# Output projection of a FoX / RG-LRU block: six layer norms' row operations on ScalarE and GpSimd, and the next layer's first weights split earlier

## The chip, the cores and the metric

The kernel runs on one core of a Trainium2 chip. The metric is the time of one launch in device microseconds (us), taken from several runs; the profile is one further execution in which every engine's instructions are recorded. The engines are PE (TensorE, the matrix engine; PEld is its loading of weights), DVE (VectorE), ACT (ScalarE), POOL (GpSimd) and SP (SyncE, which issues DMAs).

## The reference, cut to what matters

One encoder block on `x` of 1024 tokens by 1024 channels, in float32:

```python
x = layer_norm(ALPHA * x + 0.5 * swiglu(x, ffn1...), ln1_g, ln1_b)
z = x @ w_in
fox = forgetting_attention(q, k, v, fg)            # 8 heads, causal, 64 wide
lru = gelu(lg) * rg_lru(causal_depthwise_conv(lx))  # 512 channels
mix = concatenate([fox, lru]) @ w_out               # 1024 x 1024
x = layer_norm(ALPHA * x + mix, ln2_g, ln2_b)       # <- the norm that is changed
x = layer_norm(ALPHA * x + 0.5 * swiglu(x, ffn2...), ln3_g, ln3_b)

def layer_norm(x, g, b):
    mu, var = mean(x, -1), mean((x - mu)**2, -1)
    return (x - mu) * rsqrt(var + 1e-5) * g + b
```

`swiglu(x)` is `(silu(x @ w_gate) * (x @ w_up)) @ w_down` with 4096 hidden channels.

## The kernel before, in words

Every float32 product is made of three matmuls on numbers split into a high and a low part (`mm3`, lines 156 to 158: high by high, high by low, low by high). A split costs a copy on ACT (the high part) and a subtraction on DVE (the low part). The gate and up products of both feed-forward layers work on 2 by 2 blocks with seven products in place of eight, so sums and differences of blocks are formed on DVE and split there as well (`first_pair` for the first pair of weight blocks, where the blocks of `x` are formed too; `weights` for the later ones).

The stretch of the change is the end of the attention and the begin of the second feed-forward layer. The row tiles `acc[i]` (128 tokens by 1024 channels; in the rows below `row`, in the program `row_5303` for tile 7 down to `row_5296` for tile 0) hold the residual. The last two heads of the attention are finished from the last query tile to the first, and as soon as two query tiles are complete, their output projection is appended to `tiles`. `out_tile` takes one half (512 channels) of a row tile from there, multiplies (PE), adds the product to the row tile (line 222, DVE), and behind the second half runs `layer_norm` and the store of the row tile to DRAM (`x2_d`, line 1166, issued by POOL). So tiles 7, 6, 5, 4, 3, 2, 1, 0 are normalized in this order, between the attention's last steps: probabilities (lines 994 to 1003), their transposes (1014 to 1019), products with the values (1030 to 1038).

`layer_norm` computes mean and variance on DVE (lines 194, 197), a row operation (line 198: minus mean, times gain), the square root on ACT (199), four operations on one column (200 to 203: one Newton step for the inverse root) and a second row operation (205: times inverse root, plus bias). The gain tile `gb[0]` holds the negative gain, and `y` leaves line 203 negative too.

After the loop over the units, the normalized tiles 4 to 7 are transposed on PE and split into the blocks `A["11"]`, `A["12"]` (`block_1`, lines 242, 247, 248) with the rest of the `out_tile` calls between them. Then `gate_up` of the second layer begins: the first blocks of the gate and up weights (`raws`, loaded by SP) are split by `fill` (line 325), the first products follow (`x` in the rows), tiles 0 to 3 are transposed (into banks `b`, line 242), copied (line 382) and so on. `g.sum` and `u.sum` are copied to SBUF at lines 366 and 385.

Each engine executes its instructions in one fixed order. A scheduler sets that order when the program is built, from the order of the code and its own estimates; so an instruction's place on its engine can move although its line did not.

Of the kernel before, what the change touches and what calls it, by code (L numbers as in the profile page):

```python
# [17 lines left out]
P = 128  # L18
# [30 lines left out]
def f32(ap):  # L49
    return ap.bitcast(F32)  # L50


class Block:
# [133 lines left out]

    def layer_norm(self, i, done=None):

        nc, v, gb = self.nc, self.nc.vector, self.gb  # L190
        a = self.acc[i]
        st = self.small.tile([P, 2, 6], F32, tag="st", name=self.nm("st"))
        for j in range(2):
            v.bn_stats(st[:, j, :], a[:, j * H:(j + 1) * H])
        s = self.small.tile([P, 8], F32, tag="ln", name=self.nm("ln"))
        mv, sd, y, w = s[:, 0:2], s[:, 2:3], s[:, 3:4], s[:, 4:5]
        v.bn_aggr(mv, st)
        v.scalar_tensor_tensor(a, a, mv[:, 0:1], gb[0], op0=ALU.subtract, op1=ALU.mult)
        nc.scalar.activation(sd, mv[:, 1:2], AF.Sqrt, bias=self.eps)
        v.tensor_scalar(w, mv[:, 1:2], EPS, 0.5, op0=ALU.add, op1=ALU.mult)  # L200
        v.reciprocal(y, sd)
        v.scalar_tensor_tensor(w, y, w, y, op0=ALU.mult, op1=ALU.mult)
        v.scalar_tensor_tensor(y, w, 1.5, y, op0=ALU.subtract, op1=ALU.mult)
        for ds in (slice(0, H), slice(H, D)) if done else (slice(0, D),):
            v.scalar_tensor_tensor(a[:, ds], a[:, ds], y, gb[1][:, ds], op0=ALU.mult, op1=ALU.add)
            if done:
                done(i, ds)
# [59 lines left out]

    def gate_up(self, wg, wu, h_d, rows, bank, tp, wsp, raws, later=None, aside=None, js=(0, 1, 2, 3)):

# [40 lines left out]
        def first_pair(g, u):  # L310
# [22 lines left out]

            homes = {(n, m): two_blocks() for n in ("11", "21", "t1") for m in both}
            t21 = [block() for _ in range(4)]
# [15 lines left out]
            else:  # L351
                for m in both:
                    fill(m, "11", q[m][0])
                do(2)
            g.sum, u.sum = self.sum_bank(), self.sum_bank()
# [9 lines left out]
            do()  # L365
            nc.scalar.copy(g.s1, g.sum)
            fill(u, "t1", t1[u])
# [13 lines left out]
            for n, j in enumerate(js):  # L381
                nc.scalar.copy(t21[j], self.transposed(r2[j], 0, bank))
                a22[j] = self.transposed(r2[j], 1, bank)
                if n == 0:
                    nc.scalar.copy(u.s1, u.sum)
                else:
                    put(place("s1", js[n - 1]), s[js[n - 1]])
                v.tensor_tensor(s[j], a22[j], t21[j], ALU.add)
                if n:
                    do()  # L390
# [569 lines left out]
    def attention(self, w_out, mixp, ln, normed):  # L960
# [7 lines left out]
        with self.pool("att_p", 3) as pp, self.pool("att_t", 1) as tp, self.pool("att_pt", 6) as ptp, self.pool("att_qk", 2, side="right") as qkp:  # L968
# [85 lines left out]
            def out_tile():  # L1054
                i, d = tiles.pop(0)
                self.down_tile(i, list(zip(mix + [mixes[3]], w_fox)), 1.0, (d,))
                if d:
                    self.layer_norm(i)
                    normed(i)
# [38 lines left out]
def kernel(  # L1098
# [40 lines left out]
    with blk.psum():  # L1139
# [32 lines left out]
        for j in range(4):  # L1172
# [3 lines left out]
            if tiles:  # L1176
                out_tile()
        while tiles:
            out_tile()
        left.close()  # L1180
    with blk.pool("xl") as xl, blk.pool("gu_t", 4) as tp, blk.banks() as bank:
        blk.open_blocks(xl, REST)
        raws, load = blk.first_raws(ffn2_w_gate[0], ffn2_w_up[0])
        with tc.issue_after(blk.last_load.ins):
            load(0)
            load(1)
        finish = blk.gate_up(ffn2_w_gate[0], ffn2_w_up[0], h_d[1], rows, bank, tp, wsp, raws, js=(3, 2, 1, 0))
    right.close()
# [41 lines left out]
```

## Time and profile before

| | before |
|---|---|
| time, median of 3 runs | 2328.83 us (2328.11 to 2330.89) |
| time of the profiled execution | 2330.4 us |
| span of the profiled execution | 2328.7 us |
| granted TensorE clock, mean | 0.999 |
| PE busy | 2302.9 us (99% of the span), 10721 matmuls |
| DVE busy | 1632.5 us (70%), 2509 instructions |
| ACT busy | 1011.1 us (43%), 1587 instructions |
| POOL busy | 222.0 us (10%), 364 instructions |

The profiled execution's time is its span and 1.7 us around it. Busy times are sums over the instructions of an engine; the ends of matmuls are modelled, so that a busy PE can still lose some tenths of a microsecond around a wait. In the groups of rows below, "idle before" and the brackets `[0.94 <-ACT ws L382]` say for how long an engine was idle ahead of an instruction and which instruction released it.

### The profile page before, as it was taken

Reading aid. Unit: us, or ns where it says so; the run is one execution under the profiler, and the core shown is the slowest. Engines: PE = TensorE matmul, PEld = TensorE weight load, DVE = VectorE, ACT = ScalarE, POOL = GpSimd, SP = SyncE. Lnnn points to the kernel's source line nnn. Section 1 sums busy time; section 2 is a strip of 40 time slices with the busy share of each in tenths; the row PEclk is TensorE's granted clock in tenths of the full one; section 3 lists DMA queues with packets and bytes.
Section 4 is the critical chain, followed back from the end, with each engine's and each line's share of the span. In section 5 each row is a group of like instructions: output and inputs, shape, how many; then the busy total and the mean of one; then the engine's idle time right before and its main releaser. Section 6 shows DMA issues by size and latency. Waiting matters only on the chain.

```text
span 2328.7 us, 28301 instructions
## 1 busy us (share of the span) xinstructions
PE 2302.9 (99%) x10721; PEld 1916.5 (82%) x10721; DVE 1632.5 (70%) x2509; ACT 1011.1 (43%) x1587; POOL 222.0 (10%) x364
## 2 busy tenths in 40 slices
PE   9999999999999999999999899999999999999998
PEld 7888888888888888888898777888888888888887
DVE  8766665666567788866667899665656565577886
ACT  5443333334344345454456745433343333344342
POOL 0020000000000000111134510000000000000000
PEclk9999999999999999999999999999999999999999
DMA  4333232323375433232375812332323232564541
GB/s 145 121 95 125 88 118 86 118 86 118 126 263 200 167 122 122 62 109 93 106 194 145 244 55 89 102 118 86 118 89 125 94 118 86 187 245 173 181 144 73
DMA packets 175976, 298.93 MB, mean 128 GB/s; under 512 B 8208, under 2 KB 100688, under 8 KB 175840
## 3 DMA queue, kind: packets, MB, share of 16 engines
q1 hardware_dynamic: 152768, 218.16, 29.1%
q0 software_dynamic: 23072, 78.97, 9.2%
q8 instruction: 84, 1.38, 0.2%
q14 instruction: 52, 0.43, 0.1%
HBM read 214.22 MB, written 82.87 MB: 128 GB/s over the span
## 4 chain that ended last, share of the span: by engine, by line
PE 91%; DVE 5%; DMA 2%; issue 1%; ACT 1%; POOL 0%; SPq 0%; DVEq 0%; POOLq 0%; ACTq 0%
PE x L156 9%; PE x L157 9%; PE x L158 9%; PE b L156 7%; PE b L157 7%; PE b L158 7%; PE s L158 6%; PE s L157 6%; PE s L156 6%; PE a L156 5%; PE a L157 5%; PE a L158 5%; PE a L1030 1%; PE a L1014 1%; PE a L895 1%
## 5 line engine op out<-in xcount | busy, mean ns | idle before, releaser
L283 ACT CAST ws<-t 128x512 fp32r<-128x512 f32 x240 | 149.1, 624 | 394.1 <-PE b L157 266.9
L283 ACT CAST ws<-raw 128x512 fp32r<-128x512 f32 x180 | 112.0, 623 | 259.4 <-PE x L157 256.9
L284 DVE TENSOR_TENSOR ws<-raw,ws 128x512 fp32r<-128x512 f32 x180 | 123.9, 689 | 140.4 <-ACT ws L283 137.0
L284 DVE TENSOR_TENSOR ws<-t,ws 128x512 fp32r<-128x512 f32 x240 | 164.5, 686 | 70.4 <-ACT ws L283 68.5
L156 PE MATMUL b<-As,ws 128*128 128x512 f32 x512 | 199.7, 390 | 1.4 <-ACT As L319 1.0
L157 PE MATMUL a<-ws,ws 128*128 128x512 f32 x512 | 199.8, 390 | 0.3 <-DVE ws L621 0.2
L156 PE MATMUL a<-ws,ws 128*128 128x512 f32 x512 | 199.3, 390 | 0.5 <-ACT row L523 0.5
L156 PE MATMUL x<-As,ws 128*128 128x512 f32 x512 | 199.5, 390 | 0.0
L157 PE MATMUL b<-As,ws 128*128 128x512 f32 x512 | 199.5, 390 | 0.0
L158 PE MATMUL b<-As,ws 128*128 128x512 f32 x512 | 199.3, 389 | 0.0
L158 PE MATMUL x<-As,ws 128*128 128x512 f32 x512 | 199.3, 389 | 0.0
L158 PE MATMUL a<-ws,ws 128*128 128x512 f32 x512 | 199.3, 390 | 0.0
L157 PE MATMUL x<-As,ws 128*128 128x512 f32 x512 | 199.2, 389 | 0.0
L156 PE MATMUL x<-A,ws 128*128 128x512 f32 x496 | 193.7, 390 | 0.6 <-DVE row L517 0.6
L158 PE MATMUL x<-A,ws 128*128 128x512 f32 x496 | 193.2, 389 | 0.7 <-DVE ws L325 0.7
L157 PE MATMUL x<-A,ws 128*128 128x512 f32 x496 | 193.2, 389 | 0.0
L618 ACT CAST ws<-raw 128x1024 fp32r<-128x1024 f32 x112 | 117.4, 1050 | 158.8 <-PE a L157 87.9
L553 POOL DMA_DIRECT2D h_d<-row x96 | 68.8, 719 | 1149.8 <-DVE row L547 1110.7
L621 DVE TENSOR_TENSOR ws<-raw,ws 128x1024 fp32r<-128x1024 f32 x112 | 136.6, 1221 | 50.7 <-ACT ws L618 50.1
L156 PE MATMUL s<-ws,ws 128*128 128x512 f32 x384 | 149.5, 389 | 0.0
L158 PE MATMUL s<-ws,ws 128*128 128x512 f32 x384 | 149.5, 389 | 0.0
L157 PE MATMUL s<-ws,ws 128*128 128x512 f32 x384 | 149.4, 389 | 0.0
(249 smaller groups left out, 5227.8 us busy)
## 6 DMA issues: line engine op xcount, KB each, us to landing
raw<-h_d SPq DMA_DIRECT2D x56, 1024.0 KB, 5.6
h_d<-row POOLq DMA_DIRECT2D x96, 512.0 KB, 3.7
wd<-in_ffn_w_down_dram SPq DMA_DIRECT2D x32, 1024.0 KB, 7.8
raw<-in_ffn_w_gate_dram SPq DMA_DIRECT2D x30, 1024.0 KB, 5.4
raw<-in_ffn_w_up_dram SPq DMA_DIRECT2D x30, 1024.0 KB, 5.4
h_d<-row POOLq DMA_DIRECT2D x32, 256.0 KB, 2.6
raw<-in_w_in_dram SPq DMA_DIRECT2D x16, 512.0 KB, 5.1
row<-in_x_dram SPq DMA_DIRECT2D x12, 512.0 KB, 8.6
```

What stands on the lines that cost most here:

```text
L156: mm(out, ah, bh, start=first, stop=False, skip_group_check=goes_on)
L157: mm(out, ah, bl, start=False, stop=False, skip_group_check=goes_on)
L158: mm(out, al, bh, start=False, stop=last, skip_group_check=goes_on)
L283: nc.scalar.copy(hi, src)
L284: v.tensor_tensor(lo, src, f32(hi), ALU.subtract)
L553: nc.gpsimd.dma_start(d[:, 2 * n:2 * n + 2], t.rearrange("p (r t) -> p r t", r=2))
L618: cast = nc.scalar.copy(hi, src)
L621: self.mark = v.tensor_tensor(lo, src, f32(hi), ALU.subtract)
L895: nc.tensor.matmul(pa[:, 0:width], xh, wh[:, 0:width], start=k == 0, stop=False)
L1014: nc.tensor.transpose(pa[:, (j % 4) * P:(j % 4 + 1) * P], p[:, j * P:(j + 1) * P], self.ident)
L1030: mm(pv[:, ps], vt[:, j, :], pts[h, qt][j // 4][l][:, j % 4, ps], start=j == 0 and l == 0, stop=j == last and l == 1)
```

## The change

Three things change.

1. `layer_norm` has a second form, `spread=True`, used in `out_tile` for tiles 7 to 2. The two DVE row operations are gone. One operation on a column is added on DVE (`w = -mean * y`), one activation over the whole row tile on ACT (`a = a * y + w`), and two operations over the whole row tile on POOL (times `gb[0]`, plus `gb[1]`). Tiles 1 and 0 keep the old form.
2. The loads of the second layer's first raw weights and the splits of the blocks "11" of gate and up stand ahead of the last `out_tile` calls; before, the splits were made by `fill` inside `gate_up`. SP issues these loads at the same place among its other DMAs as before.
3. In the second layer's `first_pair`, the copies of `g.sum` and `u.sum` stand behind the copies of the first transposes.

The diff:

```diff
-    def layer_norm(self, i, done=None):
+    def layer_norm(self, i, done=None, spread=False):
...
         v.bn_aggr(mv, st)
-        v.scalar_tensor_tensor(a, a, mv[:, 0:1], gb[0], op0=ALU.subtract, op1=ALU.mult)
+        if not spread:
+            v.scalar_tensor_tensor(a, a, mv[:, 0:1], gb[0], op0=ALU.subtract, op1=ALU.mult)
         nc.scalar.activation(sd, mv[:, 1:2], AF.Sqrt, bias=self.eps)
         v.tensor_scalar(w, mv[:, 1:2], EPS, 0.5, op0=ALU.add, op1=ALU.mult)
         v.reciprocal(y, sd)
         v.scalar_tensor_tensor(w, y, w, y, op0=ALU.mult, op1=ALU.mult)
         v.scalar_tensor_tensor(y, w, 1.5, y, op0=ALU.subtract, op1=ALU.mult)
+        if spread:
+            v.scalar_tensor_tensor(w, mv[:, 0:1], -1.0, y, op0=ALU.mult, op1=ALU.mult)
+            nc.scalar.activation(a, a, AF.Identity, bias=w, scale=y)
+            for x, op in zip(gb, (ALU.mult, ALU.add)):
+                nc.gpsimd.tensor_tensor(a, a, x, op)
+            return
...
+    def parts(self, pool, src):
+
+        hi, lo = (pool.tile([P, 4, P], F32R, tag="ws", name=self.nm("ws")) for _ in range(2))
+        self.nc.scalar.copy(hi, src)
+        self.nc.vector.tensor_tensor(lo, src, f32(hi), ALU.subtract)
+        return hi, lo
...
-                for m in both:
-                    fill(m, "11", q[m][0])
-                do(2)
+                for m, x in zip(both, ready):
+                    m.w["11"] = x
...
-            nc.scalar.copy(g.s1, g.sum)
+            if later:
+                nc.scalar.copy(g.s1, g.sum)
...
-                if n == 0:
+                if n == (0 if later else 1):
                     nc.scalar.copy(u.s1, u.sum)
-                else:
+                if n:
                     put(place("s1", js[n - 1]), s[js[n - 1]])
+                elif not later:
+                    nc.scalar.copy(g.s1, g.sum)
...
-                    self.layer_norm(i)
+                    self.layer_norm(i, spread=i > 1)
...
+        raws, load = blk.first_raws(ffn2_w_gate[0], ffn2_w_up[0])
+        with tc.issue_after(blk.last_load.ins):
+            load(0)
+            load(1)
+        ready = [blk.parts(wsp, r[:, 0:4, 0:P]) for r in raws]
         while tiles:
             out_tile()
```

Lines below 188 move: line 222 becomes 229, 205 becomes 212, 242 becomes 249, 1003 becomes 1019, 1019 becomes 1035, 1166 becomes 1182, 325 becomes 339, 366 becomes 403, 382 becomes 396, 385 becomes 399.

**Place 1: POOL, from the norm of tile 7 to that of tile 4.** POOL works through the last attention probabilities (`p`), the masks (`cum`) and the stores of the row tiles. Before:

```order
L1166 DMA x_d<-row_5303 128x1024 [waits DMASW0_49,DVE_49]
L1003 TENSOR_SCALAR p_11490<-p_11490,m_11494 128x128 [waits DVE_49,PE_49]
L998 AFFINE_SELECT cum_11085<-cum_11085 128x128 [waits DVE_49]
L1003 TENSOR_SCALAR p_11543<-p_11543,m_11547 128x512 [waits DVE_49,PE_49]
L998 AFFINE_SELECT cum_11085<-cum_11085 128x128 [waits DVE_49]
L1003 TENSOR_SCALAR p_11593<-p_11593,m_11597 128x384 [waits DVE_49,PE_49]
...
L1166 DMA x_d<-row_5301 128x1024 [waits DMASW2_49,DVE_49]
L1166 DMA x_d<-row_5300 128x1024 [waits DMASW3_49,DVE_49]
```

and now (the probabilities of the same units are called `p_11545` and `p_11597` here):

```order
L209 TENSOR_TENSOR row_5303<-row_5303,gb_11235 128x1024 [waits Activation_49]
L1014 AFFINE_SELECT cum_11085<-cum_11085 128x128 [waits DVE_49]
L209 TENSOR_TENSOR row_5303<-row_5303,gb_11236 128x1024 [waits DMAHW1_49,Pool_49]
L1019 TENSOR_SCALAR p_11545<-p_11545,m_11549 128x512 [waits DVE_49]
L1182 DMA x_d<-row_5303 128x1024 [waits DMASW0_49,Pool_49]
L1014 AFFINE_SELECT cum_11085<-cum_11085 128x128 [waits DVE_49]
L1019 TENSOR_SCALAR p_11597<-p_11597,m_11601 128x384 [waits DVE_49,PE_49]
...
L209 TENSOR_TENSOR row_5301<-row_5301,gb_11235 128x1024 [waits DMAHW2_49,Activation_49]
L209 TENSOR_TENSOR row_5301<-row_5301,gb_11236 128x1024 [waits Pool_49]
L1182 DMA x_d<-row_5301 128x1024 [waits DMASW2_49,Pool_49]
L209 TENSOR_TENSOR row_5300<-row_5300,gb_11235 128x1024 [waits Activation_49]
L209 TENSOR_TENSOR row_5300<-row_5300,gb_11236 128x1024 [waits Pool_49]
L1182 DMA x_d<-row_5300 128x1024 [waits DMASW3_49,Pool_49]
```

Tile 7's two operations now stand ahead of a mask and of the probabilities of two units, and the operations of tiles 5 and 4 follow one another with the stores between them.

**Place 2: DVE, the norms of tiles 1 and 0.** `ws` is the low part of a weight block. Before:

```order
L222 SCALAR_TENSOR_TENSOR row_5296<-a_11994,row_5296 128x512 [waits PE_49]
L203 SCALAR_TENSOR_TENSOR ln_11957<-ln_11957 128x1 [waits DVE_49]
L194 BN_STATS st_12008<-row_5296 128x6
L205 SCALAR_TENSOR_TENSOR row_5297<-row_5297,ln_11957,gb_11236 128x1024 [waits DVE_49]
L194 BN_STATS st_12008<-row_5296 128x6
L325 TENSOR_TENSOR ws_12062<-raw_12047,ws_12061 128x512 [waits DMAHW4_49]
L197 BN_AGGR ln_12011<-st_12008 128x2 [waits DVE_49]
L325 TENSOR_TENSOR ws_12064<-raw_12046,ws_12063 128x512 [waits DMAHW5_49,Activation_49]
L198 SCALAR_TENSOR_TENSOR row_5296<-row_5296,ln_12011,gb_11235 128x1024 [waits DVE_49]
```

and now:

```order
L229 SCALAR_TENSOR_TENSOR row_5296<-a_11992,row_5296 128x512 [waits PE_49]
L204 SCALAR_TENSOR_TENSOR ln_11969<-ln_11969 128x1 [waits DVE_49]
L194 BN_STATS st_12034<-row_5296 128x6 [waits DVE_49]
L212 SCALAR_TENSOR_TENSOR row_5297<-row_5297,ln_11969,gb_11236 128x1024 [waits DMAHW1_49,DVE_49]
L229 SCALAR_TENSOR_TENSOR row_5296<-a_12020,row_5296 128x512 [waits PE_49]
L194 BN_STATS st_12034<-row_5296 128x6 [waits DVE_49]
L197 BN_AGGR ln_12037<-st_12034 128x2 [waits DVE_49]
L199 SCALAR_TENSOR_TENSOR row_5296<-row_5296,ln_12037,gb_11235 128x1024 [waits DVE_49]
```

The two splits of weight blocks are gone from this place; they and the two of the blocks "11" stand among the norms of tiles 3 and 2 now.

**Place 3: ACT, the begin of the second layer's gate and up.** Rows of `x` and `b` are PE's banks. Before:

```order
L199 ACTIVATE ln_12011<-ln_12011,eps 128x1 [waits DVE_49]
L366 COPY row_12054<-x_12079 128x512 [waits DMASW4_49,PE_49]
L385 COPY row_12054<-x_12080 128x512
L319 CAST ws_12067<-t_12093 128x512 [waits DVE_49]
L319 CAST ws_12069<-t_12096 128x512 [waits DVE_49]
L382 COPY ws_12074<-b_12126 128x512
L382 COPY ws_12073<-b_12139 128x512 [waits PE_49,Activation_49]
```

and now:

```order
L200 ACTIVATE ln_12037<-ln_12037,eps 128x1 [waits DVE_49]
L333 CAST ws_12083<-t_12105 128x512 [waits DVE_49]
L333 CAST ws_12085<-t_12108 128x512 [waits DVE_49]
L403 COPY row_12074<-x_12091 128x512 [waits DMASW4_49,PE_49,Pool_49]
L396 COPY ws_12090<-b_12137 128x512
L399 COPY row_12074<-x_12092 128x512
L396 COPY ws_12089<-b_12150 128x512 [waits PE_49,Activation_49]
```

The first copy of a transposed tile (line 382 before, 396 now) has one copy of a sum ahead of it in place of two, and the second copy of a sum follows it.

## Rows read from the trace of the kernel before

**Rows 1.** The page's busy times: engine, us, share of the span, instructions.

```profile
PE 2302.9 (99%) x10721; PEld 1916.5 (82%) x10721; DVE 1632.5 (70%) x2509; ACT 1011.1 (43%) x1587; POOL 222.0 (10%) x364
```

**Rows 2.** Stretches: length, busy us by engine, clock, DMA share, GB/s.

```profile
1390.00:1400.00 10.00, 9.34 (x44) 7.43 (x43) 9.88 (x23) 2.10 (x5) 0.53 (x1) 1.00 0.17 70
1400.00:1410.00 10.00, 8.87 (x54) 7.25 (x53) 10.00 (x16) 7.59 (x15) 0.53 (x1) 1.00 0.14 56
```

**Rows 3.** PE's waits, 1340 to 1440: us in total, times, longest.

```profile
PE b L156 <- ACT As L319: 1.0, 1, 1.0
PE b L242 <- ACT ws L382: 0.9, 1, 0.9
PE x L158 <- DVE ws L325: 0.7, 1, 0.7
PE a L158 <- DVE mix L1038: 0.3, 1, 0.3
PE a L156 <- DVE o L1034: 0.3, 1, 0.3
PE b L156 <- ACT ws L382: 0.2, 1, 0.2
```

**Rows 4.** PE in order of time: start us, us, line, tile.

```profile
1396.13 0.39 PE L156 MATMUL x<-A,ws 128*128 128x512 f32 x1
1396.36 0.39 PE L157 MATMUL x<-A,ws 128*128 128x512 f32 x1
1397.41 0.50 PE L158 MATMUL x<-A,ws 128*128 128x512 f32 x1 [0.66 <-DVE ws L325]
1397.74 0.39 PE L156 MATMUL x<-A,ws 128*128 128x512 f32 x1
...
1403.54 1.15 PE L242 MATMUL b<-ident,row 128*128 128x128 f32 x8 [0.94 <-ACT ws L382]
```

**Rows 5.** The two row operations of the norm, 1180 to 1420: ns min/median/max.

```profile
L198 DVE SCALAR_TENSOR_TENSOR row<-row,ln,gb x8: 1274/1279/1285, 1343.3 to 1397.9; 128x1024 f32<-128x1024 f32 x8
...
L205 DVE SCALAR_TENSOR_TENSOR row<-row,ln,gb x8: 1268/1280/1312, 1345.5 to 1399.8; 128x1024 f32<-128x1024 f32 x8
```

**Rows 6.** POOL's groups, 1180 to 1345: times, busy us, mean ns.

```profile
L1003 POOL TENSOR_SCALAR p<-p,m 128x1024 f32<-128x1024 f32 x8 | 9.0, 1124 | 2.2 <-PE a L1030 1.3 <-DVE m L1002 0.9
```

**Rows 7.** All engines in order of time, 1297.8 to 1299.6.

```profile
1298.10 2.32 POOL L1003 TENSOR_SCALAR p<-p,m 128x896 f32<-128x896 f32 x1
1298.33 1.21 DVE L149 TENSOR_TENSOR w<-raw,w 128x1024 fp32r<-128x1024 f32 x1
```

**Rows 8.** ACT's groups in the whole span: an activation over a row tile.

```profile
L112 ACT ACTIVATE row<-row 128x1024 f32<-128x1024 f32 x24 | 25.5, 1066 | 5.7 <-DMA row<-x_d 5.1 <-DMA row<-in_x_dram 0.6
```

**Rows 9.** All engines in order of time, tiles 5 and 4, 1362 to 1376.

```profile
1364.31 0.15 DVE L203 SCALAR_TENSOR_TENSOR ln<-ln 128x1 f32<-128x1 f32 x1
...
1370.16 0.15 DVE L203 SCALAR_TENSOR_TENSOR ln<-ln 128x1 f32<-128x1 f32 x1
...
1372.56 0.53 POOL L1166 DMA_DIRECT2D x_d<-row  x1 [5.90 <-DVE row L205]
...
1375.72 0.49 PE L242 MATMUL s<-ident,row 128*128 128x128 f32 x3
```

**Rows 10.** DVE in order of time, 1392 to 1403: tile 0's norm.

```profile
1396.68 0.67 DVE L325 TENSOR_TENSOR ws<-raw,ws 128x512 fp32r<-128x512 f32 x1
...
1397.39 0.64 DVE L325 TENSOR_TENSOR ws<-raw,ws 128x512 fp32r<-128x512 f32 x1
...
1399.84 1.28 DVE L205 SCALAR_TENSOR_TENSOR row<-row,ln,gb 128x1024 f32<-128x1024 f32 x1
```

**Rows 11.** The chain of waits, 1425 to 1440: start us, us, what.

```profile
1429.98 6.09 DMA raw<-in_ffn_w_gate_dram
...
1436.09 0.62 ACT ws L283
1436.71 0.53 ACT As L319
```

More of the change, by code (lines that the diff above doesn't have):

```diff
@@ L266, in first_raws, with gate_up @@
         return raws, load
-    def gate_up(self, wg, wu, h_d, rows, bank, tp, wsp, raws, later=None, aside=None, js=(0, 1, 2, 3)):
+    def parts(self, pool, src):
[3 more added lines that the diff above has]
+        return hi, lo
+    def gate_up(self, wg, wu, h_d, rows, bank, tp, wsp, raws, later=None, aside=None, js=(0, 1, 2, 3), ready=None):
         nc, v = self.nc, self.nc.vector
@@ L332, in fill @@
                 put(m.w[n], src)
-            homes = {(n, m): two_blocks() for n in ("11", "21", "t1") for m in both}
+            homes = {(n, m): two_blocks() for n in ("11", "21", "t1") for m in both if n != "11" or ready is None}
             t21 = [block() for _ in range(4)]
@@ L1182 @@
         blk.open_blocks(xl, REST)
[L1183 to L1187, printed above, removed]
+        finish = blk.gate_up(ffn2_w_gate[0], ffn2_w_up[0], h_d[1], rows, bank, tp, wsp, raws, js=(3, 2, 1, 0), ready=ready)
     right.close()
```

## The prediction, made before the changed kernel was run

> **What bounds the kernel now.** The page's busy times come first: PE is busy 99% of the span and DVE 70% [rows 1]. So a change can only win what PE still waits, and the first question is where these waits are. The stretches around the change show the place: in the two that hold the norms of tiles 1 and 0 and the first transposes of the second feed-forward layer, DVE is busy 9.88 and 10.00 us of 10, and PE falls to 9.34 and 8.87 [rows 2]. The granted clock is 1.00 there (2.4 GHz), so PE's loss is waiting. The list of PE's waits from 1340 to 1440 names six, all released by DVE or by ACT, 3.4 us in all [rows 3]. Where DVE has 100% of the stretch, an ACT copy that PE waits for is itself late because of DVE, through the rows that it reads or the banks that it is queued for.
>
> A wait costs more than its row says. Matmuls of one run start 0.23 us apart (1396.13, 1396.36). The one that waited for a weight split started 1.05 us after its neighbour and the next one 0.33 us later [rows 4]: 0.82 + 0.10 = 0.92 us lost where the bracket says 0.66. I take a factor of about 1.4 for each wait: the six lose some 4.6 us. **That is the most that this change can win**, and it is 0.2% of the time. About 0.2% is also what a measurement of this kernel can tell from no change (bounds 2324.2 and 2333.5).
>
> **The change part by part.**
>
> *DVE row operations removed.* Two of 1.28 us in six tiles [rows 5]: 12 x 1.28 = 15.4 us. Added: six operations on a column, 0.15 us each as line 203 [rows 9]: 0.9 us. DVE is freed of 14.5 us between 1343 and 1392. It is not the bound for this whole time (its additions wait for PE's products), so this is no gain in itself; it counts where PE waits for it.
>
> *The two waits in the attention* (lines 1034 and 1038, 0.3 us each [rows 3]) stand behind the row operations of tiles 7 to 4. With these gone DVE is ahead of PE there. With the factor: 0.9 us won.
>
> *The tail.* Before, two weight splits of 0.67 and 0.64 us stand in tile 0's norm, and its last row operation begins only at 1399.84 and ends at 1401.1 [rows 10]. Now these splits stand among the norms of tiles 3 and 2, where the removed row operations left more room than they need (4 x 0.67 = 2.7 us against 2 x 2.4). Adding up tile 0's remaining operations from the same addition, its norm ends at about 1398.3, some 2.8 us earlier. Then the wait of the matmul for the split (0.66), of the transposes for ACT's copies (0.94 [rows 4]) and the small one behind it (0.2 [rows 3]) go; the later place of the two copies of sums takes 0.6 us of ACT out of the way of the first bank as well. 1.8 us by the list, 2.4 with the loss at the restart. If the transposes still waited for a bank, 0.9 of this would stay; I take the whole.
>
> *The last wait* (1.0 us, about 1.3 with the restart [rows 3]) isn't of this kind. In the chain of waits, ACT's cast of `As` (1436.71) stands behind the cast of a weight block (1436.09), and that waited for the transfer of the next raw weights, issued at 1429.98 when DVE had freed their buffer, 6.09 us long [rows 11]. The transfer keeps its length; it starts earlier by what DVE is earlier, some 3.4 us (2.8 and the 0.6 that PE, and with it the addition, is earlier by then). PE itself is earlier by 3.0. So only the difference is won, 0.3 to 0.6; I take 0.3. Bounds: 0 and 1.3.
>
> *ACT's added work.* Six activations over a row tile, 1.07 us each [rows 8], 6.4 us, where ACT is busy 2 to 8 of 10 us [rows 2]. It costs nothing where a PE-bound copy isn't directly behind it; that cover gone, one collision delays a copy by up to 1.07 us.
>
> *POOL's added work* decides. Twelve operations with two inputs in SBUF over 128x1024; the trace before has none. Nearest row: one input, 1.12 us [rows 6]. The longest row of POOL's kind is 2.32 us, for 128x896 beside a DVE operation with two inputs [rows 7]. Bounds: 1.12 (a second input costs nothing) and 2 x 2.32 = 4.64 (both reads at the slow rate). I take 2 x 1.12 = 2.25: the undisturbed row [rows 6], once for each input. The Trainium skill (GPSIMD Engine Reference, § 3.1 Elementwise) gives 4497 ns for such an operation of twice this length, which would make an estimate of 2.25 too; no run here shows it yet.
>
> With 2.25 the tightest place is tile 4, the first that PE transposes. Before, its norm ends ahead of the store at 1372.56, and PE wants it at 1375.72 [rows 9]: 3.2 us of room. Now tile 5's column `w` is ready at about 1364.3 (where line 203 ran before [rows 9]; its DVE operation is released by PE, not by the row operations), the activation ends at 1365.4, two POOL operations at 1369.9, the store's issue takes 0.53 [rows 9]: 1370.4. Tile 4's `w` is ready before 1370.2 (line 203 ran at 1370.16 behind a row operation that is gone), so its activation has ended by then, and its two POOL operations end at 1374.9. PE, 0.9 us earlier by the attention's waits, wants the tile at 1374.8 to 1375.2. So this is just met or just missed: I put 0.3 us of waiting here. Four POOL operations stand in that chain: each 0.1 us beyond about 2.35 costs 0.4 us of PE.
>
> Ahead of that, the pair of tile 7 stands before a mask and the probabilities of two units (place 1 of the order). The added 2 x 2.25 us delay these; PE transposes those probabilities units later, and I put nothing on it. Were that cover gone, it would be up to 2.25 us once.
>
> The sum: 0.9 + 2.4 + 0.3 - 0.3 = 3.3 us. The profiled execution takes 2330.4 us, 1.6 above the median 2328.83; off its own time it gives 2327.1, off the median **2325.5 us**. Behind 1440 nothing of the change is left, and PE, which is the bound, carries the shift to the end.
>
> **The rivals.**
>
> *GpSimd's operation is slower (ends on the other side).* Place: PE's transposes of tile 4. Beyond 2.35 us the price is 4 x (t - 2.35). At t = 3.25 the 3.6 us won elsewhere (0.9 + 2.4 + 0.3) are eaten; at the bound of 4.64, PE waits 9 us, and the time is 2328.8 - 3.6 + 9.2 = 2334.4. For it: an operation that by its size should take 1.12 x 896 / 1024 = 0.98 us stretched to 2.32 beside DVE [rows 6, 7], and DVE stays busy. Against it: DVE's operations with two SBUF inputs are few now (the splits, the mix, columns), since the row operations that would stretch POOL are those removed. Chance 0.09.
>
> *DVE is blocked by POOL.* If a DVE operation with two inputs in SBUF waits for the POOL operation that is under way, then each of the twelve holds DVE for half its length on average, 12 x 1.1 = 13.5 us against the 14.5 freed. DVE is as late as before, the waits stay, tile 4's chain is later by a few tenths for each of its column operations: 2328.8 to 2333, about 2330.5. Against it: DVE's operation that began 0.23 us into a POOL operation took 1.21 us, no longer than a row operation without one (1.27), and POOL's was the one that stretched [rows 5, 7]. The Trainium skill (SBUF — State Buffer, § Who interferes with whom) states the rule: whoever issues first has the shared ports for the whole instruction, and the other is fully blocked. By that rule DVE should have waited in this pair, and the row disagrees. Chance 0.09.
>
> *Nothing arrives.* The tail's gain is given back at the last wait: the transfer of raw weights starts no earlier, because its issue hangs on something else than DVE, or the added activations delay ACT's copies by as much. Then PE waits 3 us longer at 1437: 2328, between 2327 and 2330. For it: the 6.09 us transfer is the longest piece there [rows 11]. Against it: DVE is full from 1400 to 1410 [rows 2], so all it does follows its start. Chance 0.12.
>
> **How the numbers follow.** The forecast has 0.70; its own range is 2323.8 to 2327.3 (all the waits gone; or one bank's wait and 0.9 us at tile 4 kept). Range for 8 in 10: 2323.7 to 2330.5, which takes in the third rival and the near half of the second. Faster than 2324.2 needs every wait won: a quarter of the forecast's chance, 0.17. Slower than 2333.5: half of the first rival, the far end of the second and what I haven't seen, 0.10. Same: 0.73.
>
> **What the profile after would show.** Row operations on POOL of about 2.25 us; no wait of PE at the transposes of tile 4 above 0.5 us; none for the weight split of 1397 and for the bank at 1403; DVE's stretches from 1350 to 1390 below 9 of 10; the raw weights' transfer issued 3 us earlier and a last wait of less than 1 us. A POOL operation above 3 us, DVE operations with two inputs that last 2 us, or a new wait of PE for `row` would make the prediction wrong.

## The result, and the profile after

The changed kernel takes 2333.55 us (median of 20 runs, 2331.20 to 2337.85), the kernel before 2329.28 us in the same session (20 runs, 2327.12 to 2331.45). The ratio is 1.0018 with a 95% interval of [1.0012, 1.0024]: **slower by 4.3 us**, clear of zero and a little less than the 0.2% that the prediction took as its bound. The prediction had 2325.5 us, with a range from 2323.7 to 2330.5.

PE's busy time by the page is 1.2 us above that of [rows 1], and the span has grown by 5.2 us; so most of the loss is waiting.

```profile
span 2333.9 us, 28314 instructions
PE 2304.1 (99%) x10721; PEld 1918.7 (82%) x10721; DVE 1626.9 (70%) x2503; ACT 1018.1 (44%) x1593; POOL 251.1 (11%) x376
```

PE's waits after, 1340 to 1450, to be set beside [rows 3] (`mix` is the split output of the attention, which the output projection multiplies; `A` the split of the transposed rows):

```profile
PE s L249 <- DVE A L255: 3.1, 2, 2.8
PE a L158 <- DVE mix L1054: 1.9, 1, 1.9
PE b L249 <- ACT ws L396: 1.3, 2, 0.9
PE b L156 <- ACT As L333: 1.0, 1, 1.0
```

The wait for the weight split (0.7) is gone as predicted. The bank's wait and the last one stayed, and two large ones are new, both released by DVE. The stretches show what is odd about them (length, busy us of PE, PEld, DVE, ACT, POOL, clock):

```profile
1360.00:1370.00 10.00, 8.21 (x43) 6.49 (x41) 7.80 (x20) 4.41 (x8) 7.88 (x6) 1.00 0.13 52
1370.00:1380.00 10.00, 9.90 (x41) 8.13 (x42) 6.26 (x18) 4.25 (x8) 5.99 (x5) 0.83 0.26 105
1380.00:1390.00 10.00, 6.95 (x34) 5.33 (x33) 9.18 (x14) 3.94 (x8) 5.65 (x3) 0.87 0.13 54
```

PE waits for DVE where DVE has room (7.80 of 10), and the clock has fallen. DVE's timeline shows how:

```profile
1367.25 0.22 DVE L203 SCALAR_TENSOR_TENSOR ln<-ln 128x1 f32<-128x1 f32 x1
1367.50 2.21 DVE L204 SCALAR_TENSOR_TENSOR ln<-ln 128x1 f32<-128x1 f32 x1
1369.63 0.41 DVE L1054 TENSOR_TENSOR mix<-o,mix 128x256 fp32r<-128x256 f32 x1
...
1375.09 0.69 DVE L229 SCALAR_TENSOR_TENSOR row<-a,row 128x512 f32<-128x512 f32 x1 [2.63 <-PE a L158]
1375.82 0.69 DVE L194 BATCH_NORM_STATS2 st<-row 128x6 f32<-128x512 f32 x1
...
1381.15 1.73 DVE L279 TENSOR_TENSOR ws<-raw,ws 128x512 fp32r<-128x512 f32 x1
1382.81 2.88 DVE L339 TENSOR_TENSOR ws<-raw,ws 128x512 fp32r<-128x512 f32 x1
```

An operation on one column (line 204) lasts 2.21 us; the same operation took 0.15 before (line 203 in [rows 9]). Two weight splits last 1.73 and 2.88 us; such splits took 0.67 and 0.64 before [rows 10]. POOL's timeline beside it, where each row is the pair of operations (times gain, plus bias) of one row tile:

```profile
1364.83 4.87 POOL L209 TENSOR_TENSOR row<-row,gb 128x1024 f32<-128x1024 f32 x2 [1.40 <-ACT row L207]
...
1371.48 4.84 POOL L209 TENSOR_TENSOR row<-row,gb 128x1024 f32<-128x1024 f32 x2 [0.89 <-ACT row L207]
...
1379.95 5.19 POOL L209 TENSOR_TENSOR row<-row,gb 128x1024 f32<-128x1024 f32 x2 [2.74 <-ACT row L207]
```

The column operation ends at 1369.71, and POOL's pair at 1369.70. Line 339 ends at 1385.69, 0.55 us behind the pair that ends at 1385.14; line 279 at 1382.88, some 0.5 us behind the middle of that pair. All three read two tensors in SBUF. Beside tile 4's pair (1371.48 to 1376.32), an addition with one input in PSUM (line 229) and the norm's statistics with a single input (line 194) keep their 0.69 us. POOL's operation itself is near its estimate (2.40 for 2.25), and ACT's a little longer than in [rows 8]:

```profile
L209 POOL TENSOR_TENSOR row<-row,gb x12: 2364/2398/2730, 1347.3 to 1394.8; 128x1024 f32<-128x1024 f32 x12
...
L207 ACT ACTIVATE row<-row,ln x6: 1227/1242/1247, 1346.0 to 1391.0; 128x1024 f32<-128x1024 f32 x6
```

Behind each wait PE is slow, which PE's timeline shows by the distance of its starts:

```profile
1370.10 0.56 PE L158 MATMUL a<-w,mix 128*128 128x512 f32 x1 [1.89 <-DVE mix L1054]
...
1371.95 0.63 PE L156 MATMUL a<-w,mix 128*128 128x512 f32 x1
1372.38 0.63 PE L157 MATMUL a<-w,mix 128*128 128x512 f32 x1
...
1374.20 0.40 PE L156 MATMUL a<-w,mix 128*128 128x512 f32 x1
1374.43 0.39 PE L157 MATMUL a<-w,mix 128*128 128x512 f32 x1
...
1388.13 1.12 PE L249 MATMUL s<-ident,row 128*128 128x128 f32 x4 [2.76 <-DVE A L255]
```

0.43 us apart at 1372, 0.23 at 1374. The granted clock (the figure behind the count) was 0.50 from 1371 to 1373, that is 1.2 GHz, and 0.53 from 1389 to 1391, each time behind an idle PE:

```profile
1371.00:1373.00 2.00, 2.00 (x6) 0.50 0.64 262
...
1389.00:1391.00 2.00, 2.00 (x9) 0.53 0.00 0
```

Eight matmuls at 0.43 cost 8 x 0.20 = 1.6 us, the second time about 1.0.

The account by places: at 1332.5 the two kernels start the same matmul within 0.06 us; the first product of the second layer starts at 1393.41 before and at 1400.18 after, 6.8 us later (the two waits 2.1 + 2.9 + 0.3 beyond the normal distance, the clock 2.6, less the 0.8 won in the attention, make 7.1); behind it 1.1 us come back by 1450 and 0.4 near 2000, where nothing was changed, and 5.2 are left at the end. This is the account of the profiled execution, 2.4 us above the median: the seven of the 20 runs whose mean granted clock was 0.996 or 0.997, this one among them, took 2335.20 to 2337.85 us, and the thirteen at 0.998 or 0.999 took 2331.20 to 2334.37, so that the fall of the clock is a part of the loss in some runs and not in all.

### The profile page after: what moved, and what is told of

It is laid out like the page before. It is cut to its first block, busy times and chain, and to the rows that moved or that the text cites. A ratio compares the mean times of both kernels' runs of the same rounds, so it can differ in the third digit from the quotient of the medians.

```text
span 2333.9 us, 28314 instructions
## 1 busy us (share of the span) xinstructions
PE 2304.1 (99%) x10721; PEld 1918.7 (82%) x10721; DVE 1626.9 (70%) x2503; ACT 1018.1 (44%) x1593; POOL 251.1 (11%) x376
## 4 chain that ended last, share of the span: by engine, by line
PE 93%; DVE 4%; issue 1%; DMA 1%; ACT 1%; POOL 0%; SPq 0%; DVEq 0%; POOLq 0%; ACTq 0%
PE x L156 10%; PE x L158 10%; PE x L157 10%; PE b L156 7%; PE b L157 7%; PE b L158 7%; PE s L158 6%; PE s L157 6%; PE s L156 6%; PE a L156 6%; PE a L158 6%; PE a L157 6%; PE a L1046 1%; PE a L1030 1%; PE a L911 1%
```

## The experiments

Theory A: a VectorE operation with two inputs in SBUF is blocked while a GpSimd operation that reads SBUF is under way. Theory B: the order of the instructions, or the weight splits put ahead, are at fault. Times are medians of 5 to 11 runs; each ratio is to the kernel before in the same session (2329.5 to 2330.0), so differences between two changed kernels of different sessions are rough. Each edit also lets the scheduler move some instructions; therefore the rows are read beside the times. A "pair" is GpSimd's two operations on one row tile, and "blocked" is an operation that lasts longer while the other engine's is under way.

**norms_only** is the kernel before with part 1 of the change alone.

```diff
...
-                    self.layer_norm(i)
+                    self.layer_norm(i, spread=i > 1)
```

> The kernel before, with the row operations of the six norms on ScalarE and GpSimd and nothing else of the change. Theory A (a VectorE operation with two inputs in SBUF waits until GpSimd's operation on a row tile has ended): column operations of the norms and the split of the mix still last up to 2.4 us in place of 0.15 to 0.4, TensorE still waits 1 to 2 us for the mix of the last head, and the time is 1 to 5 us above the kernel before; the wait of 2.8 us for the split of the transposed rows is smaller, since the weight splits don't stand ahead of it, but some VectorE operation is blocked there too. Theory B (the order of the instructions is at fault, above all the weight splits that were moved ahead): no wait over 0.5 us, and the time is that of the kernel before or up to 3 us less.

2331.09 us, ratio 1.0007 [0.9998, 1.0015]: 1.4 us above the kernel before, which isn't clear of zero. The rows are clear: the column operation is stretched to 2.21 us and PE waits 1.9 for the mix, as A has it (DVE's timeline, then PE's waits); one weight split, that of the old place, takes 1.67.

```profile
1369.72 2.21 DVE L204 SCALAR_TENSOR_TENSOR ln<-ln 128x1 f32<-128x1 f32 x1
...
PE a L158 <- DVE mix L1045: 1.9, 1, 1.9
```

Here the clock stayed at 1.00 behind the wait, so that its fall isn't certain.

**splits_only** is the changed kernel without part 1.

```diff
-                    self.layer_norm(i, spread=i > 1)
+                    self.layer_norm(i)
```

> The changed kernel with all eight norms in the old form on VectorE: only the weight splits ahead of the last tiles and the later copies of the sums are left of the change. Theory A: no VectorE operation is stretched, and the time is within 2 us of the kernel before (the wait for the weight split of 0.7 us and that of the bank of 0.9 us may go, the splits cost 2.7 us of VectorE among norms that fill it). Theory B: TensorE waits 2 us or more for the split of the transposed rows, as in the changed kernel, and the time is 2 to 5 us above the kernel before.

2329.69 us, ratio 1.0002 [0.9993, 1.0011]. No operation is stretched and B's wait isn't there (0.3). So parts 2 and 3 do no harm alone, and win nothing: the wait for the weight split is gone, PE reaches the transposes earlier and waits there instead.

```profile
PE b L249 <- ACT ws L396: 2.0, 1, 2.0
```

The clock is at 0.50 from 1404 to 1406 behind that wait. Part 1 alone costs 1.4 us and the other two nothing, against 4.3 together. What they cost together fits the second place in the changed kernel, where GpSimd's pair of tile 3 blocks two of the moved weight splits ahead of the split of the transposed rows.

**gpsimd_write_only** takes away GpSimd's reading and keeps its time.

```diff
-            for x, op in zip(gb, (ALU.mult, ALU.add)):
-                nc.gpsimd.tensor_tensor(a, a, x, op)
+            for x in (1.0, 2.0, 1.0, 2.0, 1.0):
+                nc.gpsimd.memset(a, x)
```

> The changed kernel with GpSimd's two operations on each row tile replaced by five constant fills of the same row tile: the same waits for the activation, about the same time on GpSimd (5 fills of some 1 us), but it reads nothing. The gain and the bias of the six tiles are left out, and their rows are constants. Theory A: no VectorE operation with two inputs is stretched (column operations 0.15 to 0.25 us, weight splits 0.7 us), both large waits of TensorE are under 0.5 us, the clock stays at 1.00, and the time is 2324 to 2327. Theory B, and also a theory by which GpSimd's duration matters: the waits for the mix and for the split stay, 2331 to 2335.

2327.07 us, ratio 0.9987 [0.9978, 0.9996], 6.5 us below the changed kernel (of another session). GpSimd's row work takes as long as in the changed kernel (28.6 us here, 12 x 2.40 = 28.8 there):

```profile
L209 POOL MEMSET row<- 128x1024 f32 x30 | 28.6, 954 | 6.0 <-ACT row L207 4.9
```

No operation is stretched, the clock stays at 1.00, and PE's waits are short (lines 204 and 339 on DVE, then PE's waits):

```profile
1374.26 0.16 DVE L204 SCALAR_TENSOR_TENSOR ln<-ln 128x1 f32<-128x1 f32 x1
...
1377.79 0.68 DVE L339 TENSOR_TENSOR ws<-raw,ws 128x512 fp32r<-128x512 f32 x1
...
PE b L249 <- ACT ws L396: 0.9, 2, 0.6
PE b L156 <- ACT As L333: 0.6, 1, 0.6
PE s L249 <- DVE A L255: 0.2, 1, 0.2
```

This decides between A and B: it is GpSimd's reading and not its time. It isn't the order either: up to the first of the weight splits DVE's instructions stand in the order of the changed kernel. From there the splits have changed places, and there the stretched rows of the changed kernel decide: 1.73 and 2.88 us in place of 0.7 each are 3.2 us, more than PE's wait of 2.8. The run also measures what the move could win without the block: 2.6 us, with an interval from 0.9 to 5.1, where the prediction had 3.3.

**columns_one_input**, and **norms_columns** (the same edit on norms_only), take the column operations out of the blocked kind.

```diff
-        v.scalar_tensor_tensor(w, y, w, y, op0=ALU.mult, op1=ALU.mult)
-        v.scalar_tensor_tensor(y, w, 1.5, y, op0=ALU.subtract, op1=ALU.mult)
         if spread:
-            v.scalar_tensor_tensor(w, mv[:, 0:1], -1.0, y, op0=ALU.mult, op1=ALU.mult)
+            v.tensor_scalar(w, y, w, y, op0=ALU.mult, op1=ALU.mult)
+            v.tensor_scalar(y, w, 1.5, y, op0=ALU.subtract, op1=ALU.mult)
+            v.tensor_scalar(w, mv[:, 0:1], y, -1.0, op0=ALU.mult, op1=ALU.mult)
...
```

> The changed kernel; the three column operations of the inverse root and of minus mean times root take one tensor and per-partition scalars in place of two tensors. The result is the same. Theory A, in the form that two tensor inputs are what is blocked: no column operation lasts over 0.3 us, the wait for the mix falls from 1.9 us to under 0.8 (the split of the mix itself has two inputs), the clock stays at 1.00 around 1370; the weight splits are still blocked, with the wait of about 2.8 us for the split of the transposed rows; the time falls by 2 to 4 us against the changed kernel, to about that of the kernel before. Theory B: nothing changes, 2333 to 2335.

> The kernel before with the six norms in the new form and columns of one tensor; no earlier splits, no later copies of the sums. The result is the same. The block theory: no column operation over 0.3 us; the mix's split of the last values is blocked in its place, by up to 2.4 us, and TensorE waits up to 1.3 us for tile 4's rows; against norms_only (2331.1) 0 to 2 us less: 2329 to 2331.

2330.59 us, ratio 1.0003 [0.9994, 1.0012], and 2328.79 us, ratio 0.9999 [0.9990, 1.0008]. No column operation is over 0.3 us and the wait for the mix is gone: 3.0 us below the changed kernel and 2.3 below norms_only, across sessions (the intervals of the second two overlap). The expected wait of 2.8 us for the split of the transposed rows fell to 0.7, which the expectation didn't have: tile 3's pair begins 3.4 us earlier than in the changed kernel, and one weight split alone is blocked by it (1.67 us). What has two inputs is still blocked: in columns_one_input the last split of the mix ends 0.3 us behind POOL's pair (DVE's and POOL's timelines).

```profile
1371.87 2.38 DVE L1058 TENSOR_TENSOR mix<-o,mix 128x256 fp32r<-128x256 f32 x1
...
1369.13 4.84 POOL L213 TENSOR_TENSOR row<-row,gb 128x1024 f32<-128x1024 f32 x2
```

PE also waits 1.3 us for tile 4's rows in both, the place that the prediction feared:

```profile
PE s L253 <- POOL row L213: 1.3, 1, 1.3
```

**pair_alone** has GpSimd and VectorE alone.

```diff
+        phase(f"A{rep}", two(2), d_two(256), 6 + 8 * rep)
...
+        phase(f"C{rep}", two(2), d_one, 6 + 8 * rep)
+        phase(f"D{rep}", two(2), d_bank, 6 + 8 * rep)
+        phase(f"E{rep}", fills, d_two(256), 6 + 8 * rep)
+        phase(f"F{rep}", late, d_two(D, 4), 0)
+        phase(f"G{rep}", two(2), d_two(1), 14 + 4 * rep)
...
```

> GpSimd and VectorE alone, nothing of the block is computed and the output is zeros. In each phase ScalarE releases both; GpSimd runs two row operations of 128x1024 with two inputs in SBUF (phases A, C, D, G), four of them (I), the two as eight pieces of 256 columns (B, H), five constant fills (E), or one that starts while VectorE is at work (F). VectorE runs, some 1 to 2 us into that, one operation of 128x256 with two inputs in SBUF (A, B, E, I), six of them (H), four of 128x1024 (F), one of 128x1 (G), one with one input (C), one with an input in PSUM and one in SBUF (D). The second round starts VectorE later. Theory A, one block for one GpSimd instruction: the operation of A ends at the end of the GpSimd instruction under way, 0.4 us of work later; in B it waits less than 0.7 us; in C, D and E it lasts its usual 0.3 to 0.45; in F GpSimd's operation is the one that is stretched. Theory A, the block lasts as long as GpSimd has the next instruction ready: in A and B it ends with the last of GpSimd's instructions (up to 4.5 us), in I up to 9 us. A rival (a slower memory for both, no block): operations in A and B last up to twice as long, and GpSimd's too.

POOL's and DVE's timelines (the letter behind p or g is the phase):

```profile
17.26 4.76 POOL L92 TENSOR_TENSOR pC<-pC,gain 128x1024 f32<-128x1024 f32 x2 [1.67 <-ACT gC L81]
...
37.12 3.00 POOL L106 TENSOR_TENSOR pF<-pF,gain 128x1024 f32<-128x1024 f32 x1
44.30 4.76 POOL L92 TENSOR_TENSOR pG<-pG,gain 128x1024 f32<-128x1024 f32 x2 [4.18 <-ACT gG L81]
...
70.12 4.76 POOL L92 TENSOR_TENSOR pA<-pA,gain 128x1024 f32<-128x1024 f32 x2 [1.67 <-ACT gA L81]
...
84.02 4.76 POOL L92 TENSOR_TENSOR pC<-pC,gain 128x1024 f32<-128x1024 f32 x2 [2.01 <-ACT gC L81]
```
```profile
18.28 1.47 DVE L115 TENSOR_SCALAR dx<-dx,gC 128x256 f32<-128x256 f32 x1
...
24.70 0.48 DVE L118 SCALAR_TENSOR_TENSOR dx<-bank,gD,dy 128x256 f32<-128x256 f32 x1
...
31.13 0.48 DVE L111 SCALAR_TENSOR_TENSOR dx<-dx,gE,dy 128x256 f32<-128x256 f32 x1
...
36.64 7.20 DVE L111 SCALAR_TENSOR_TENSOR dx<-dx,gF,dy 128x1024 f32<-128x1024 f32 x4 [5.02 <-ACT gF L81]
...
46.83 2.25 DVE L111 SCALAR_TENSOR_TENSOR dx<-dx,gG,dy 128x1 f32<-128x1 f32 x1
...
72.65 2.52 DVE L111 SCALAR_TENSOR_TENSOR dx<-dx,gA,dy 128x256 f32<-128x256 f32 x1
...
86.20 0.35 DVE L115 TENSOR_SCALAR dx<-dx,gC 128x256 f32<-128x256 f32 x1
```

0.48 us is the operation beside fills (E) or with an input in PSUM (D). Beside reading row operations it lasts 2.52 and ends 0.29 us behind POOL (A, second round; in the first it began as POOL's first operation ended, and lasted 0.48); one column, 2.25 (G). Beside four row operations in a row (I) it lasts 1.60 and 2.52: the block lasts for one instruction of GpSimd, not for all of its queue. In F both lose: POOL's operation, started under way of DVE's first, takes 3.00 in place of 2.38, and DVE's four take 7.20 in place of 4 x 1.28 = 5.1. The miss is C: an operation of 256 columns with one input was blocked too. In the first round it took 1.47 us and ended 0.1 us behind the middle of POOL's pair; in the second it took 0.35, but it began only 0.2 us ahead of that middle, so this round can't show that it was free. So two inputs in SBUF aren't the whole condition. Columns of one input weren't blocked: the one-column operations that delay DVE in these phases keep their 0.15 us beside POOL.

**gpsimd_quarters**, **quarters_columns**, **quarters_not_tile4** and **quarters_norms_only** cut GpSimd's operations in four.

```diff
-                nc.gpsimd.tensor_tensor(a, a, x, op)
+                for c in range(0, D, 256):
+                    nc.gpsimd.tensor_tensor(a[:, c:c + 256], a[:, c:c + 256], x[:, c:c + 256], op)
```

> The changed kernel with each of GpSimd's operations on a row tile in four pieces of 256 columns. The result is the same. Theory A in the form that the block lasts for one instruction of GpSimd (not for all its queued work): no VectorE operation is stretched by more than 0.7 us (a piece's length), the column operation ahead of the mix ends 1.5 us earlier, the waits of 1.9 and 2.8 us fall below 0.8 each and the clock stays at 1.00 there; GpSimd's time grows by some 0.1 us per piece, so tile 4 may come 1 us late; time 2326 to 2331. If the block lasted as long as GpSimd has work, the stretches and the time (2333 to 2335) stay.

> As gpsimd_quarters, and the column operations take one tensor and scalars. The result is the same. Theory A: what is still blocked are the mix's split, the weight splits and the old row operations of tiles 1 and 0, by up to 0.7 us each; 0 to 2 us faster than gpsimd_quarters, 2326 to 2330.

> As quarters_columns, but tile 4, the first that TensorE transposes, keeps the old form on VectorE (two row operations of 1.28 us). The result is the same. Theory A: no wait of TensorE for GpSimd's rows; VectorE's two row operations are blocked by at most a piece each; 2325 to 2329. If VectorE's own time were what counts there, the two row operations bring back a wait of 0.3 us for the mix.

> As quarters_columns without the earlier weight splits and without the later copies of the sums: the kernel before with the six norms in the new form, columns of one tensor, GpSimd in pieces. The result is the same. Theory A: no weight splits among the norms to be blocked; the waits for the mix and for the split of the transposed rows are under 0.5 us each; 2325 to 2329, at or below quarters_columns.

2337.35, 2335.66, 2333.68 and 2337.64 us; ratios 1.0035 [1.0022, 1.0047], 1.0032 [1.0020, 1.0045], 1.0015 [1.0006, 1.0024], 1.0035 [1.0023, 1.0048]. All four times lie above their ranges, by 4.7 to 8.6 us. The pieces cost 5.6 us per tile and more in place of 4.8, and PE waits up to 2.4 us for POOL's rows in three of the four (not in quarters_not_tile4, as expected). PE also waits 2.1 to 2.4 us ahead of the first product of the second layer, for an addition that stands behind other work in DVE's order; how much of this is block isn't separated. The block got shorter for some: in gpsimd_quarters no column operation lasts over 0.69 us, and the wait for the mix is 0.3. But the mix's last split isn't let in: in quarters_columns it lasts until POOL's last piece has ended, six pieces on, and in gpsimd_quarters and quarters_norms_only it does the same (3.66 and 4.36 us).

```profile
1375.07 4.34 DVE L1059 TENSOR_TENSOR mix<-o,mix 128x256 fp32r<-128x256 f32 x1
...
1373.57 5.56 POOL L214 TENSOR_TENSOR row<-row,gb 128x256 f32<-128x256 f32 x8
```

**pieces_offsets** asks for that alone.

```diff
+    for n, delay in enumerate((2, 5, 8, 11, 14, 17)):
+        phase("ABCDEF"[n], pieces, split(256), delay)
+        phase("KLMNOP"[n], pieces, split(512), delay)
+        phase("QRSTUV"[n], two(2), split(256), delay)
```

> GpSimd and VectorE alone again; nothing of the block is computed, the output is zeros. One operation of VectorE with two inputs in SBUF and a rounded output (as the mix's split) starts at six offsets into GpSimd's work: phases A to F 128x256 against eight pieces, K to P 128x512 against eight pieces, Q to V 128x256 against two whole row operations. If the block always ends at the end of GpSimd's instruction: no operation of A to F lasts over 0.7 + 0.5 us, none of K to P over 0.7 + 0.7, those of Q to V last up to 2.4 + 0.5, depending on the offset. If a release at a boundary is a matter of chance or of what else runs: some of A to F last 1.4 us or more.

The longest operation beside pieces is this one (DVE's timeline):

```profile
97.57 1.25 DVE L128 SCALAR_TENSOR_TENSOR lo<-t,gO,hi 128x512 fp32r<-128x512 f32 x1
```

So DVE was let in at the next piece or the one behind it each time; beside whole operations it lasted up to 2.52. Why the mix was shut out for five and six pieces in the kernel isn't settled.

**tiles_7_6**, **tiles_7_6_3_2**, **norms_7632** and **norms_not_4** give only some tiles the new form (columns of one tensor; the last two without parts 2 and 3); **one_gpsimd_operation** moves half of each norm.

The diff is that of tiles_7_6, cut to the choice of tiles.

```diff
...
-                    self.layer_norm(i, spread=i > 1)
+                    self.layer_norm(i, spread=i > 5)
```

> The changed kernel with the new form of the norm for tiles 7 and 6 alone, and the column operations with one tensor there. The result is the same. Theory A: GpSimd's four operations lie ahead of 1363, where VectorE has few operations with two inputs; no stretched operation, no wait of TensorE over 0.5 us ahead of 1390; behind that VectorE is as full as in the kernel before, so the bank's wait (2.0 us with the splits alone) stays; time 2327 to 2330.

> As tiles_7_6, and the new form for tiles 3 and 2 too: tiles 5 and 4, whose GpSimd operations blocked the mix, keep the old form. The result is the same. Theory A: the mix waits 0.3 us at most; weight splits may still be blocked by tile 3's operations (up to 2.4 us, with a wait of 0.5 to 1.2 us for the split of the transposed rows); the bank's wait shrinks to below 1 us; time 2325 to 2329.

> As norms_columns, with tiles 5 and 4 in the old form. The result is the same. The block theory: tile 5's first row operation is blocked by tile 6's GpSimd operations (2.9 us in place of 1.28), a weight split or a split of transposed rows by tile 3's (1.7 to 2.9 us); without the four splits close together TensorE's wait is 0.5 to 1.5 us in place of 3.1; 2329 to 2332.

> As norms_columns, with tile 4 alone in the old form. The result is the same. The block theory: tile 5's GpSimd operations block the mix's split or tile 4's first row operation by up to 2.4 us; no wait for GpSimd's rows; 2328 to 2332. A time below 2327 would say that a share of the move pays.

> The six norms with half of the move: VectorE keeps the first row operation (minus mean, times gain), ScalarE multiplies by the inverse root, GpSimd only adds the bias (one operation per tile in place of two). The result is the same. Theory A: GpSimd's share of the time, and with it the chance of a block, is halved: fewer stretched operations and one wait of about 1 us at most; VectorE has half of its time back; 2326 to 2331. If only the freed time of VectorE counted, it would lie halfway between the changed kernel (2333.5) and the kernel before (2329.3) or above.

2330.52, 2335.39, 2333.53, 2331.79 and 2331.95 us; ratios 1.0004 [0.9995, 1.0013], 1.0024 [1.0014, 1.0034], 1.0016 [1.0008, 1.0025], 1.0010 [1.0001, 1.0019], 1.0010 [1.0001, 1.0019]. None is faster than the kernel before, and all but norms_not_4 lie above their ranges. tiles_7_6 was to have no stretched operation, and has one: an old row operation of tile 5, now behind tile 6's pair (which ends at 1362.05), takes 2.93 us in place of 1.28.

```profile
1360.20 2.93 DVE L199 SCALAR_TENSOR_TENSOR row<-row,ln,gb 128x1024 f32<-128x1024 f32 x1
```

In tiles_7_6_3_2 the moved weight splits are blocked (1.87 and 2.88 us) and PE waits 3.1 for the transposed rows' split; with one GpSimd operation per tile, two of them take 3.50 together and PE waits 1.7. In norms_7632 tile 5's row operation (2.96) and two splits (2.45 and 1.67) are blocked, as expected, and PE waits 1.9 for the transposed rows' split (0.5 to 1.5 were expected); in norms_not_4 the mix's split is (2.42), and PE waits 2.5 for it. So each variant has its block elsewhere. The block isn't all of their loss: in all but norms_not_4, PE waits 1.2 to 2.5 us ahead of the first product of the second layer. In tiles_7_6 that is its longest wait (1.2), and GpSimd's last row operation ended over 30 us earlier; there it is no block of that moment, and the addition that it waits for stands behind other work in DVE's order.

## Why the prediction was wrong

**The step that failed** is in the second rival, "DVE is blocked by POOL", under "Against it": that DVE's operation, begun 0.23 us into a POOL operation, lasted 1.21 us and so didn't wait [rows 7]. The row was read too far. POOL's operation there took 2.32 us where the seven others of its size in that trace took 1.01 or 1.02 (the prediction's estimate was 0.98): it was stretched by 1.3 us, about the length of DVE's operation, and ended 0.9 us behind it. One of the two had shut the other out, and by these lengths it was DVE that had the memory, although POOL's row begins first. Two rows that start within 0.23 us don't tell who came first at the memory, and POOL's stretch was evidence of a block, not against one. The trace before has a second such pair (all engines in order of time):

```profile
1288.56 1.21 DVE L149 TENSOR_TENSOR w<-raw,w 128x1024 fp32r<-128x1024 f32 x1
...
1288.81 1.41 POOL L1003 TENSOR_SCALAR p<-p,m 128x384 f32<-128x384 f32 x1 [0.56 <-DVE m L1002]
```

Here DVE began first, and POOL's operation took 1.41 us where the others of its size took 0.58 or 0.59. The one that came second waited; in the changed kernel that is DVE.

The Trainium skill (SBUF — State Buffer, § Who interferes with whom) states that a DVE instruction with two SBUF inputs contends with a GpSimd instruction that reads SBUF, not with one that only writes it. The runs agree: 0.48 us beside fills, 2.52 beside reads. The row that the prediction set against the rule doesn't contradict it.

The rival had 0.09, and by these rows deserved most of the chance; the sum held no term for it. "DVE operations with two inputs that last 2 us", which the prediction named as a sign that it would be wrong, came.

**Its price was too low as well**: 2330.5 against 2333.55. It was taken as a mean delay of DVE, and its own range ended at 2333. In the profiled execution the loss came from blocks at two places ahead of operations that PE waits for, and from what followed: 5 us of idle PE, and 2.6 us at the lower clock behind it, which no term held.

Point by point. POOL's operation was taken at 2.25 us and measured 2.40. ACT's activation was taken at 1.07 and measured 1.24. Tile 5's pair was put at 1365.4 to 1369.9 and ran from 1364.83 to 1369.70. Tile 4's didn't follow at once: one of its column operations was the blocked one, so that its pair began at 1371.48, and PE, late itself, didn't wait for it. The first rival (GpSimd too slow) didn't come true in the changed kernel; with the columns freed, its wait appeared (1.3 us, where the rival's price for 2.40 us is 4 x 0.05 = 0.2). The ceiling of 4.6 us is 1.4 x 3.4 = 4.8 when worked out; nothing hangs on it.

The gain was probably over-sized. Without the block (gpsimd_write_only) the attention's waits (0.9 us) and that for the weight split did go. The tail's 2.4 us contained the bank's wait, which stays at 0.9 even there, and the last wait stays at 0.6. The time says 2.6 us, whose interval still holds 3.3. That the weight splits moved alone only hand their wait to the next bank (0.7 and 0.9 us before, 2.0 then) wasn't in the prediction either.

## What to carry to other kernels

Moving row work from VectorE to GpSimd frees VectorE only while the operations that stay on it and that TensorE waits for aren't of the kind that GpSimd's reading blocks: a column operation of 0.15 us lasted 2.2 us there. Before such a move, list VectorE's operations with two SBUF inputs in that stretch; one input alone is no safe sign, since a one-input operation of 256 columns was blocked too. Column arithmetic can often be written with one tensor and per-partition scalars, which took back 2 to 3 us here. And a wait of TensorE is to be priced with the lower clock that may follow it.

## What the hardware showed that was not expected

Beside GpSimd's operations cut into pieces of 0.7 us, one VectorE operation lasted 3.66, 4.34 and 4.36 us in three kernels, up to the end of the last piece, while alone no operation beside the same pieces lasted over 1.25. Beside whole operations alone, the blocked VectorE operations of 128x256 with two inputs ended 0.2 to 0.3 us behind GpSimd's instruction, where they take 0.48 us without a block; whether a part of that time had passed during the wait, or they were let in ahead of the recorded end, the rows don't tell. And TensorE's clock fell to 0.50 for 2 to 3 us behind waits of 1.9 and 2.8 us in the changed kernel, and behind one of 2.0 in splits_only, but stayed at 1.00 behind waits of 1.9 us in norms_only and 2.5 us in norms_not_4.
